# One hybrid decoder layer on one core: causal attention taken in pairs of heads, score products alternating between the two 64-row halves of the array, and the same for the GLA state products

## The chip, the cores and the metric

The kernel runs on one core of a Trainium2 chip. The metric is the device time of one launch in microseconds. The kernel before takes 718.95 us, the median of three runs (718.24 to 720.07).

## What is computed

One decoder layer on 512 tokens of width 1024, all in float32 at the interface. What the change touches are two of its parts; both read the same RMS-normed input:

```python
# 8 attention heads of width 64, causal, blocks of 256 keys, T5 bias by distance
s_own = einsum('hqd,hld->hql', qi, k_own) * scale + table_t[:, rel_bucket(d_own)]
...
p = softmax(concatenate([s_sel, s_own], axis=-1))
o_a = einsum(p_sel, v_sel) + einsum(p_own, v_own)
# 4 heads of gated linear attention: key width 64, value width 128
o_inter = einsum('bhcd,bhde->bhce', qf * exp(b), S)
o_intra = einsum('bhij,bhje->bhie', A, vf)
o_g = rms_norm(o_inter + o_intra, g_norm) * silu(rg)
x = x + concatenate([o_a, o_g]) @ w_out
```

With 512 tokens and blocks of 256, every past block is chosen, so the attention is plain causal attention. After it come an output projection with a residual sum, cross-attention over 256 memory tokens, and a squared-ReLU MLP, none of which the change touches.

## The kernel before, in words

Dense products are made in three passes of half-precision parts (high by high, high by low, low by high), each a matmul of 128 rows by up to 512 columns (`gemm_steps`, L227 to L229, and `gemm_tok_steps`, L242 to L244). One step of such a product is three matmuls. TensorE's order is the order of the program text; the other engines' instructions are ordered by the framework's own planner.

To keep TensorE busy while other engines work between dependent products, independent products are kept in a queue of generators, `fill`, and `fill(n)` issues n steps of them. Where a dependent product stands in TensorE's order is thus set by the number of fill steps written ahead of it.

**GLA** (class `Gla`) works on the four heads in two pairs. Head hh of a pair lies in rows 64 hh to 64 hh + 63 of the pair's tiles. For each head `outp` makes the output of four token tiles J in one PSUM bank: a float32 product of 128 rows with the local matrix `adg` (L643), and for J > 0 a float32 product of 64 rows with the state handed on, `st` (L645). A float32 product shows as two matmul instructions in the trace. The squares go to ScalarE (L647), and `norm` sums them with a matmul (L652), takes the root through `rstd_neg2`, and scales the output (L656). The loop calls, for each head, `outp`, four fill steps, `norm`, three fill steps. Earlier, `small`, `mid` and `large` (L562, L571, L580) make the local matrices with small products whose position alternates between the two row halves.

**Attention.** `Head` works on one head. It loads the bias rows (L723) and spreads them with GpSimd (L724). `score(qt)` makes the scores of one block of 128 queries against its 128 (qt + 1) keys in one PSUM bank: three matmuls of 64 rows (L732 to L734). Then VectorE adds the bias and takes the row maximum (L737, L738), and ScalarE the exponentials with their sum (L740). After the blocks 2 and 0, `parts` splits two blocks of probabilities into half-precision parts, high on ScalarE (L759), low on VectorE (L760). When all four are there, `trans` issues one transposing DMA for the head (L764). Two heads later `attn_out(p)` (L775) multiplies the transposed probabilities of the two heads of pair p with the values, in matmuls of 128 rows by 64 columns that alternate between the two column halves; `split` (L273, L274) puts the result into `mix[p]`.

The main loop (L828 to L851) runs over the heads: the query blocks 3, 2, 1, 0 with one fill step after each (two from the second head on, for g > 0), then `trans`; after every second head from the fourth on `attn_out` of the pair that is two heads back. The fill queue holds the projections of the later heads (`qk_steps`), the gates (`rg_steps`), and from the ninth round on the first part of the output projection (`early_steps`, which reads `mix[0]`, `mix[1]`, `mix[4]`, `mix[5]`) and the rest of it (`residual_steps`). The last `attn_out` has six early and three more steps ahead of it in the last rounds, and one behind it.

PSUM has five banks for such work (`sbank`, L64) and three for the dense products (`gbank`). The transposed probabilities have three buffers.

Of the kernel before, what the change touches and what calls it, by code (L numbers as in the profile page):

```python
# [9 lines left out]
F16 = mybir.dt.float16  # L10
# [6 lines left out]
P = 128  # L17
# [12 lines left out]
# pairs of tiles (f, f + 16) of the hidden layer in the order they are made, for each half of the second  # L30
# product's contraction: (plain,), or (by seven products, plain alongside or None)
# [7 lines left out]
def hybrid_block_kernel(  # L39
# [10 lines left out]
    # ---------------------------------------------------------------- pools  # L50
# [16 lines left out]
    # ------------------------------------------------------------ constants  # L67
# [16 lines left out]
    # ------------------------------------------------------- weight streams  # L84
    class Weights:
# [16 lines left out]
        def pieces(self, n):  # L102
            """the next weight tile in n column ranges, one at a time"""
# [116 lines left out]
    # matmuls of one output tile, three passes of half-precision parts per K tile  # L220
# [26 lines left out]
    # independent products that fill the tensor engine between dependent ones  # L247
# [28 lines left out]
    # (v y^2 - 3) y = -2 rsqrt(v): one Newton step on y = exp(-ln(v)/2), v = ssq / dim  # L276
# [12 lines left out]
    def norm_steps(xs, n, gcol, dst, c0, ssq, nm, inplace=False, keep=None):  # L289
        """dst[kt][:, h/l, c0:c0+n] = split(xs[kt] * rstd * gain)"""  # L290
# [11 lines left out]
    class SumSq:  # L302
        """sum over the features of the squares, plus 1024 * EPS"""
# [38 lines left out]
    # ------------------------------------------------------ phase-1 storage  # L342
# [13 lines left out]
    # --------------------------------------------------- norms of mem and x  # L356
    # mem * gain is split as it comes; its 1/rms is applied to the products
# [83 lines left out]
    # ------------------------------------------------ GLA input projections  # L441
# [54 lines left out]
    # ------------------------------------------------------------------ GLA  # L496
    class Gla:
# [26 lines left out]
        # blocks of 8 tokens: both exponents are taken from the block's middle  # L524
# [10 lines left out]
        # left half against right half of blocks of 2 s tokens, exponents from the end of the left  # L535
# [65 lines left out]
        # between tiles of 128 tokens  # L601
# [19 lines left out]
        # what the tiles before hand on: st[J] = exp(b at the end) st[J - 1] + kc^T v  # L621
# [14 lines left out]
        def outp(self, hh):  # L636
            h = 2 * self.pr + hh
            ps = self.po = sbank(f"go{h}")
            vc = slice(h * P, h * P + P)
            r = slice(64 * hh, 64 * hh + 64)  # L640
# [5 lines left out]
            self.sq = pg.tile([P, T], F32, tag="gd", bufs=2, name=f"gsq{h}")  # L646
            ACT.activation(self.sq, ps, AF.Square)  # L647

        def norm(self, hh):
            h = 2 * self.pr + hh  # L650
            pv = sbank(f"gss{h}")
            PE.matmul(pv, ones, self.sq, start=True, stop=True)  # L652
# [3 lines left out]
            DVE.scalar_tensor_tensor(mixf[4 + h], self.po, gneg[:, G_GN:G_GN + 1], w, op0=ALU.mult, op1=ALU.mult)  # L656
# [3 lines left out]
    # --------------------------------------------------------------- T5 bias  # L660
    # vector over distances, copied to 128 rows of DRAM that shift by one each
# [21 lines left out]
    for pr in range(2):  # L683
# [31 lines left out]
    # ----------------------------------------------------- causal attention  # L715
# [3 lines left out]
    class Head:  # L719
        def __init__(self, h):  # L720
            self.h, self.r, self.pr = h, slice(64 * (h % 2), 64 * (h % 2) + 64), {}
            bq = self.bq = p1.tile([P, T], F32, tag="bq", bufs=3, name=f"bq{h}")
            nc.sync.dma_start(bq[:, 256:], bscr[h, :, 127:383])  # L723
# [24 lines left out]
        def parts(self, qt):  # L748
            # key block kt of query block qt lies at qt + 3 kt, the last one at 7
            if qt == 3:  # L750
                self.pq = pt.tile([P, 2, 10, P], F16, tag="pq", bufs=2, name=f"pq{self.h}")
# [590 lines left out]
```

## Time and profile before

| What | Value |
|---|---|
| Runs | 718.24, 718.95, 720.07 us |
| Span of the profiled execution, first to last instruction | 715.9 us |
| Time of the profiled execution beyond its span | not listed; the median is 3.0 us above the span |
| TensorE busy | 693.4 us, 97% of the span |
| VectorE busy | 553.9 us, 77% |
| ScalarE busy | 419.6 us, 59% |
| GpSimd busy | 84.5 us, 12% |
| Granted TensorE clock, mean | 0.989 of full speed |
| Share of the chain that ended last on TensorE | 81% |

The share of the chain says which engine the end waited for; the busy share says only how often an engine had work. A stretch of matmuls is read best from the starts in the timeline: the time from one start to the next is what a matmul takes from the stream, while its own duration also holds the way through the array, which the next one overlaps.

### The profile page before, as it was taken

Reading aid. Unit: us, or ns where it says so; the run is one execution under the profiler, and the core shown is the slowest. Engines: PE = TensorE matmul, PEld = TensorE weight load, DVE = VectorE, ACT = ScalarE, POOL = GpSimd, SP = SyncE. Lnnn points to the kernel's source line nnn. Section 1 sums busy time; section 2 is a strip of 40 time slices with the busy share of each in tenths; the row PEclk is TensorE's granted clock in tenths of the full one; section 3 lists DMA queues with packets and bytes.
Section 4 is the critical chain, followed back from the end, with each engine's and each line's share of the span. In section 5 each row is a group of like instructions: output and inputs, shape, how many; then the busy total and the mean of one; then the engine's idle time right before and its main releaser. Section 6 shows DMA issues by size and latency. Waiting matters only on the chain.

```text
span 715.9 us, 13482 instructions
## 1 busy us (share of the span) xinstructions
PE 693.4 (97%) x5370; PEld 473.8 (66%) x5370; DVE 553.9 (77%) x1003; ACT 419.6 (59%) x803; POOL 84.5 (12%) x97
## 2 busy tenths in 40 slices
PE   6997999999999999999999999999999999999995
PEld 3843455554333488788888854458888866488884
DVE  7899762747889918857639899889878889999825
ACT  6686544538888617455536666555444766665533
POOL 5701000200110024200124100000000000003211
PEclk8999999999999999999999999999999999999998
DMA  8766623006585903326403332203333342314003
GB/s 315 253 215 206 253 80 103 2 2 224 129 185 132 248 33 119 118 60 177 104 16 122 115 108 70 89 30 119 118 122 114 122 165 70 117 49 139 21 1 119
DMA packets 56628, 85.63 MB, mean 120 GB/s; under 512 B 32075, under 2 KB 37492, under 8 KB 56564
## 3 DMA queue, kind: packets, MB, share of 16 engines
q1 hardware_dynamic: 56564, 84.76, 38.1%
q8 instruction: 42, 0.69, 0.4%
q14 instruction: 22, 0.18, 0.1%
HBM read 75.30 MB, written 3.68 MB: 110 GB/s over the span
## 4 chain that ended last, share of the span: by engine, by line
PE 81%; DVE 11%; ACT 3%; issue 2%; DMA 1%; POOL 1%; DVEq 0%; SPq 0%; ACTq 0%; POOLq 0%
PE up L228 6%; PE up L229 6%; PE up L227 6%; PE a L1116 4%; PE a L1118 4%; PE a L1117 4%; DVE whl L115 3%; PE qk L227 2%; PE qk L229 2%; PE qk L228 2%; PE xq L227 2%; PE xq L229 2%; PE xq L228 2%; PE c L1117 2%; PE c L1118 2%
## 5 line engine op out<-in xcount | busy, mean ns | idle before, releaser
L115 DVE SCALAR_TENSOR_TENSOR whl<-wst,whl 128x1024 f16<-128x1024 f32 (+1 forms) x162 | 197.5, 1226 | 32.1 <-ACT whl L114 31.6
L114 ACT ACTIVATE whl<-wst 128x1024 f16<-128x1024 f32 (+1 forms) x162 | 165.6, 1028 | 33.1 <-PE a L1118 8.0
L227 PEld LDWEIGHTS <-whl 128*128 128x128 f16 x784 | 77.0, 98 | 47.8 <-issue 9.6
L229 PEld LDWEIGHTS <-whl 128*128 128x128 f16 x784 | 77.0, 98 | 46.6 <-DVE whl L115 3.3
L228 PEld LDWEIGHTS <-whl 128*128 128x128 f16 x784 | 77.2, 98 | 36.4 <-issue 1.0
L227 PE MATMUL up<-act,whl 128*128 128x512 f16 (+1 forms) x224 | 78.1, 349 | 0.0
L228 PE MATMUL up<-act,whl 128*128 128x512 f16 (+1 forms) x224 | 78.1, 349 | 0.0
L229 PE MATMUL up<-act,whl 128*128 128x512 f16 (+1 forms) x224 | 78.1, 349 | 0.0
L1116 PE MATMUL a<-t,whl 128*128 128x256 f16 x192 | 52.3, 273 | 1.1 <-ACT v L1133 1.1
L1118 PE MATMUL a<-t,whl 128*128 128x256 f16 x192 | 52.3, 273 | 0.0
L1117 PE MATMUL a<-t,whl 128*128 128x256 f16 x192 | 52.3, 273 | 0.0
L1117 PEld LDWEIGHTS <-whl 128*128 128x128 f16 x456 | 44.6, 98 | 6.9 <-issue 1.5
L1116 PEld LDWEIGHTS <-whl 128*128 128x128 f16 x456 | 44.6, 98 | 5.2
L1118 PEld LDWEIGHTS <-whl 128*128 128x128 f16 x456 | 44.6, 98 | 5.0
L228 PE MATMUL xq<-act,whl 128*128 128x256 f16 x128 | 34.9, 273 | 0.2 <-DVE act L274 0.2
L228 PE MATMUL xo<-ox,whl 128*128 128x256 f16 x128 | 34.9, 273 | 0.0
L227 PE MATMUL xo<-ox,whl 128*128 128x256 f16 x128 | 34.9, 273 | 0.0
L229 PE MATMUL xo<-ox,whl 128*128 128x256 f16 x128 | 34.9, 273 | 0.0
L227 PE MATMUL xq<-act,whl 128*128 128x256 f16 x128 | 34.9, 273 | 0.0
L229 PE MATMUL xq<-act,whl 128*128 128x256 f16 x128 | 34.9, 273 | 0.0
L273 ACT ACTIVATE t<-hs 128x512 f16<-128x512 f32 x32 | 19.8, 624 | 23.9 <-DVE hs L998 23.7
L321 POOL TENSOR_SCALAR accf<-accf 128x128 f32<-128x128 f32 (+1 forms) x3 | 3.5, 1166 | 249.5 <-ACT accf L311 249.5
(339 smaller groups left out, 1722.4 us busy)
## 6 DMA issues: line engine op xcount, KB each, us to landing
wst<-in_w_up SPq DMA_DIRECT2D x32, 512.0 KB, 3.8
wst<-in_w_down SPq DMA_DIRECT2D x32, 512.0 KB, 4.1
wst<-in_w_tt SPq DMA_DIRECT2D x16, 512.0 KB, 4.1
wst<-in_w_xv SPq DMA_DIRECT2D x8, 512.0 KB, 5.2
wst<-in_w_vv SPq DMA_DIRECT2D x8, 512.0 KB, 4.3
wst<-in_w_out SPq DMA_DIRECT2D x8, 512.0 KB, 3.8
wst<-in_w_xq SPq DMA_DIRECT2D x8, 512.0 KB, 3.8
wst<-in_w_xo SPq DMA_DIRECT2D x8, 512.0 KB, 4.6
```

The source lines that it names most:

```text
L114: ACT.activation(wt[:, 0, c], stg[:, c], AF.Copy, scale=SW)
L115: DVE.scalar_tensor_tensor(wt[:, 1, c], stg[:, c], SW, wt[:, 0, c], op0=ALU.mult, op1=ALU.subtract)
L227: PE.matmul(ps, wt[:, 0, kt, :], a[:, 0, c0:c1], start=st, stop=False, **kw)
L228: PE.matmul(ps, wt[:, 0, kt, :], a[:, 1, c0:c1], start=False, stop=False, **kw)
L229: PE.matmul(ps, wt[:, 1, kt, :], a[:, 0, c0:c1], start=False, stop=sp, **kw)
L273: ACT.activation(dst_h, src, AF.Copy, scale=scale)
L321: POOL.tensor_scalar(self.acc, self.acc, 1024 * EPS / P, None, op0=ALU.add)
L1116: PE.matmul(ps, w[:, 0, kt, :], b[:, 0, c], start=st, stop=False, skip_group_check=not start)
L1117: PE.matmul(ps, w[:, 0, kt, :], b[:, 1, c], start=False, stop=False, skip_group_check=not start)
L1118: PE.matmul(ps, w[:, 1, kt, :], b[:, 0, c], start=False, stop=sp, skip_group_check=not start)
```

## The change

`Gla.outp` makes both heads of a pair in one call: first all eight products with `adg` (128 rows), then the six with the state, J by J, the two heads in turn, in two banks. The fill steps around it are regrouped: six behind `outp`, four behind each `norm`, so 14 for a pair as before. In the attention, `Head` becomes `Pair`: for a query block the three score passes of the two heads alternate between the row halves, in two PSUM banks. The small operations on the maxima and sums work on two columns at once. Scores and probabilities share one buffer for each query block. The bias tile of a pair moves to another pool. `trans` issues two transposing DMAs, one behind the other. Between the query blocks stand two fill steps where there was one for each head; two more follow `trans`; and `attn_out` of a pair comes within the next pair's round, behind its third query block.

```diff
-        def outp(self, hh):
-            ps = self.po = sbank(f"go{h}")
...
-            for J in range(4):
-                o = ps[:, J * P:J * P + P]
-                PE.matmul(o, vg[J][:, vc], self.adg[:, hh * 4 + J, :], start=True, stop=(J == 0))
-                if J > 0:
-                    PE.matmul(o, self.st[r, J * P - P:J * P], self.qb[r, J * P - P:J * P], start=False, stop=True)
+        def outp(self):
+            self.po = [sbank(f"go{2 * self.pr + hh}") for hh in range(2)]
+            for hh in range(2):
+                h = 2 * self.pr + hh
+                for J in range(4):
+                    PE.matmul(self.po[hh][:, J * P:J * P + P], vg[J][:, h * P:h * P + P], self.adg[:, hh * 4 + J, :],
+                              start=J == 0, stop=False, skip_group_check=True)
+            for J in range(1, 4):
+                for hh in range(2):
+                    r = slice(64 * hh, 64 * hh + 64)
+                    PE.matmul(self.po[hh][:, J * P:J * P + P], self.st[r, J * P - P:J * P], self.qb[r, J * P - P:J * P],
+                              start=False, stop=J == 3, skip_group_check=True)
...
+        G.outp()
+        fill(6)
         for hh in range(2):
-            G.outp(hh)
+            G.norm(hh)
             fill(4)
-            G.norm(hh)
-            fill(3)
...
-    class Head:
+    class Pair:
...
+            bq = self.bq = pt.tile([P, 2, T], F32, tag="bq", bufs=2, name=f"bq{p}")
...
         def score(self, qt):
-            ps = sbank(f"s{h}_{qt}")[:, :n]
-            PE.matmul(ps, aq[p][r, 0, qs], ak[p][r, 0, :n], start=True, stop=False)
-            PE.matmul(ps, aq[p][r, 0, qs], ak[p][r, 1, :n], start=False, stop=False)
-            PE.matmul(ps, aq[p][r, 1, qs], ak[p][r, 0, :n], start=False, stop=True)
+            pss = [sbank(f"s{p}_{qt}_{hh}")[:, :n] for hh in range(2)]
+            for i, (a, b) in enumerate(((0, 0), (0, 1), (1, 0))):
+                for hh, ps in enumerate(pss):
+                    r = slice(64 * hh, 64 * hh + 64)
+                    PE.matmul(ps, aq[p][r, a, qs], ak[p][r, b, :n], start=i == 0, stop=i == 2)
...
+                self.pq = [pt.tile([P, 2, 10, P], F16, tag="pq", bufs=3, name=f"pq{self.p}_{hh}") for hh in range(2)]
...
         def trans(self):
+            self.ph = []
+            for hh in range(2):
+                pT = pt.tile([P, 20, P], F16, tag="pT", bufs=3, name=f"pT{self.p}_{hh}")
+                nc.sync.dma_start(pT, self.pq[hh].rearrange("p s n t -> p (s n t)"), transpose=True)
...
-    for i in range(10):
+    for i in range(5):
...
         for g in range(4):
-            if i < 8:
-                heads[i].score(3 - g)
-                fill(1)
-            if g > 0 and 1 <= i <= 8:
-                fill(1 if i < 8 else 2)
-        if i < 8:
-            heads[i].trans()
-        if i == 9:
-            fill(3)
-        if i >= 3 and i % 2 == 1:
-            p = (i - 3) // 2
-            attn_out(p, [heads.pop(2 * p), heads.pop(2 * p + 1)])
-            fill(1)
+            if i < 4:
+                pairs[i].score(3 - g)
+                fill(2)
+            if g > 0 and i >= 1:
+                fill(2 if i < 4 else 4)
+            if 1 <= i < 4 and g == 2:
+                attn_out(pairs.pop(i - 1))
+        if i < 4:
+            pairs[i].trans()
+            fill(2)
+    fill(3)
+    attn_out(pairs.pop(3))
+    fill(1)
```

## Rows read from the trace of the kernel before

**Rows 1.** The page's first part: busy time and instructions of each engine.

```profile
PE 693.4 (97%) x5370; PEld 473.8 (66%) x5370; DVE 553.9 (77%) x1003; ACT 419.6 (59%) x803; POOL 84.5 (12%) x97
```

**Rows 2.** Busy time by stretch (start:end, length, engines, PEclk, DMA share, GB/s): the attention.

```profile
175.00:250.00 75.00, 75.00 (x416) 29.93 (x416) 67.95 (x213) 58.84 (x140) 3.72 (x5) 1.00 0.74 181
```

**Rows 3.** TensorE's timeline (start, duration, what) around the first `outp`, then L643's durations.

```profile
117.31 0.38 PE L244 MATMUL va<-whl,act 128*128 128x512 f16 x1
117.53 0.61 PE L643 MATMUL go<-adg,vgs 128*128 128x128 f32 x4
118.06 0.49 PE L645 MATMUL go<-qb,st 64*128 64x128 f32 x2
118.48 0.49 PE L643 MATMUL go<-adg,vgs 128*128 128x128 f32 x2
...
120.15 0.39 PE L242 MATMUL va<-whl,act 128*128 128x512 f16 x1
...
L643 PE MATMUL go<-adg,vgs x32: 273/275/377, 117.5 to 168.2; 128*128 128x128 f32 x32
```

**Rows 4.** TensorE's timeline through the four score groups of the first head.

```profile
174.69 0.38 PE L229 MATMUL qk<-act,whl 128*128 128x512 f16 x1
175.00 0.39 PE L732 MATMUL s<-qks,qks 64*128 64x512 f16 x1
...
175.75 0.39 PE L227 MATMUL qk<-act,whl 128*128 128x512 f16 x1
...
176.19 0.38 PE L229 MATMUL qk<-act,whl 128*128 128x512 f16 x1
...
177.09 0.39 PE L227 MATMUL qk<-act,whl 128*128 128x512 f16 x1
...
177.54 0.38 PE L229 MATMUL qk<-act,whl 128*128 128x512 f16 x1
...
178.28 0.39 PE L227 MATMUL qk<-act,whl 128*128 128x512 f16 x1
...
178.72 0.38 PE L229 MATMUL qk<-act,whl 128*128 128x512 f16 x1
...
179.30 0.39 PE L227 MATMUL qk<-act,whl 128*128 128x512 f16 x1
```

**Rows 5.** TensorE's timeline, matmuls begun within 0.02 and 0.01 us: alternating row halves, column halves.

```profile
102.06 0.27 PE L580 MATMUL ps<-z 64*64 64x64 f32 x2
...
201.05 0.41 PE L775 MATMUL o<-pT,vas 128*64 128x512 f16 x2
```

**Rows 6.** Softmax chain by tile: count, duration min/median/max in ns, first and last start.

```profile
L740 ACT ACTIVATE p<-ss,sm x32: 384/553/723, 179.2 to 235.0; 128x512 f32<-128x512 f32 x8, 128x384 f32<-128x384 f32 x8, 128x256 f32<-128x256 f32 x8, 128x128 f32<-128x128 f32 x8
...
L759 ACT ACTIVATE pq<-p,sm x40: 384/502/616, 182.5 to 239.0; 128x384 f16<-128x384 f32 x16, 128x128 f16<-128x128 f32 x16, 128x256 f16<-128x256 f32 x8
...
L764 SPq DMA_TRANSPOSE pT<-pq x8: 3017/3284/4232, 185.3 to 240.5; - x8
...
DMA to landing us min/median/max: 4.9/5.4/6.6
```

**Rows 7.** Timeline: last score groups of the sixth and eighth head, their transposes, the last `attn_out`.

```profile
215.88 0.23 PE L732 MATMUL s<-qks,qks 64*128 64x128 f16 x1
...
220.13 3.02 SPq L764 DMA_TRANSPOSE pT<-pq  x1
...
232.38 0.23 PE L732 MATMUL s<-qks,qks 64*128 64x128 f16 x1
...
240.47 4.23 SPq L764 DMA_TRANSPOSE pT<-pq  x1
...
247.56 0.41 PE L775 MATMUL o<-pT,vas 128*64 128x512 f16 x2
```

**Rows 8.** Busy time by stretch (columns of rows 2): a long wait of TensorE, and the stretch behind it.

```profile
58.20:62.20 4.00, 0.51 (x11) 0.18 (x11) 4.00 (x8) 3.23 (x5) 0.00 (x0) 1.00 0.77 262
62.20:65.60 3.40, 3.10 (x19) 0.76 (x17) 3.40 (x5) 2.65 (x5) 0.00 (x0) 0.50 0.38 114
```

More of the change, by code (lines that the diff above doesn't have):

```diff
@@ L651, in norm @@
             pv = sbank(f"gss{h}")
-            PE.matmul(pv, ones, self.sq, start=True, stop=True)
+            PE.matmul(pv, ones, self.sq[hh], start=True, stop=True)
             v = pg.tile([P, T], F32, tag="gd", bufs=2, name=f"gv{h}")
@@ L655, in norm @@
             w = rstd_neg2(v, T, 1.0, f"g{h}")
-            DVE.scalar_tensor_tensor(mixf[4 + h], self.po, gneg[:, G_GN:G_GN + 1], w, op0=ALU.mult, op1=ALU.mult)
+            DVE.scalar_tensor_tensor(mixf[4 + h], self.po[hh], gneg[:, G_GN:G_GN + 1], w, op0=ALU.mult, op1=ALU.mult)
     for _ in gqk_steps(0):
@@ L717, in hybrid_block_kernel, with __init__ @@
     pt = s3.enter_context(tc.tile_pool(name="patt", bufs=1, reuse_waits="tile"))
-    class Head:
[L720 to L723, printed above, removed]
-            POOL.tensor_copy(bq[:, :256], bq[:, 256:257].to_broadcast([P, 256]))
-            self.sm = pt.tile([P, 12], F32, tag="sm4", bufs=3, name=f"sm4_{h}")
+    class Pair:
+        def __init__(self, p):
+            self.p, self.pr = p, {}
+            bq = self.bq = pt.tile([P, 2, T], F32, tag="bq", bufs=2, name=f"bq{p}")
+            for hh in range(2):
+                nc.sync.dma_start(bq[:, hh, 256:], bscr[2 * p + hh, :, 127:383])
+                POOL.tensor_copy(bq[:, hh, :256], bq[:, hh, 256:257].to_broadcast([P, 256]))
+            self.sm = pt.tile([P, 3, 4, 2], F32, tag="sm4", bufs=2, name=f"sm4_{p}")
@@ L735, in score @@
-            s = pt.tile([P, T], F32, tag="s", bufs=3, name=f"ss{h}_{qt}")[:, :n]
-            mx, ng, sm = (self.sm[:, 4 * i + qt:4 * i + qt + 1] for i in range(3))
-            DVE.tensor_tensor_reduce(s, ps, self.bq[:, T - n:], scale=1.0, scalar=NEG, op0=ALU.add, op1=ALU.max, accum_out=mx)
+            for i, (a, b) in enumerate(((0, 0), (0, 1), (1, 0))):
+                for hh, ps in enumerate(pss):
+                    r = slice(64 * hh, 64 * hh + 64)
+                    PE.matmul(ps, aq[p][r, a, qs], ak[p][r, b, :n], start=i == 0, stop=i == 2)
@@ L738, in score @@
+            mx, ng, sm = (self.sm[:, i, qt, :] for i in range(3))
+            for hh, ps in enumerate(pss):
+                s = self.pr[qt, hh] = pt.tile([P, n], F32, tag=f"p{qt}", bufs=2, name=f"p{p}_{qt}_{hh}")
+                DVE.tensor_tensor_reduce(s, ps, self.bq[:, hh, T - n:], scale=1.0, scalar=NEG, op0=ALU.add, op1=ALU.max, accum_out=mx[:, hh:hh + 1])
             DVE.tensor_scalar(ng, mx, -1.0 / (SA * SA), None, op0=ALU.mult)
-            pr = self.pr[qt] = pt.tile([P, T], F32, tag="p", bufs=4, name=f"p{h}_{qt}")[:, :n]
@@ L740, in score @@
-            ACT.activation(pr, s, AF.Exp, bias=ng, scale=1.0 / (SA * SA), accum_out=sm)
+            for hh in range(2):
+                s = self.pr[qt, hh]
+                ACT.activation(s, s, AF.Exp, bias=ng[:, hh:hh + 1], scale=1.0 / (SA * SA), accum_out=sm[:, hh:hh + 1])
             if qt % 2 == 0:
-                r = self.sm[:, 8 + qt:10 + qt]
+                r = self.sm[:, 2, qt:qt + 2, :]
                 DVE.reciprocal(r, r)
@@ L775, in attn_out @@
                     PE.matmul(ps[64 * hh:64 * hh + 64, P * kt:T], va[kt][:, a, 64 * h:64 * h + 64],
-                              heads[hh].ph[:, b, offs[kt]:offs[kt] + n],
+                              pair.ph[hh][:, b, offs[kt]:offs[kt] + n],
                               start=(kt == 0 and a == 0 and b == 0), stop=(kt == 3 and a == 1),
@@ L827, in hybrid_block_kernel @@
     fill.add(qk_steps(2), qk_steps(3), *[rg_steps(h) for h in range(4)])
-    heads = {}
-    for i in range(10):
-        if i < 8:
-            heads[i] = Head(i)
-        if i in (4, 6):
-            fill.until({4: 5, 6: 4}[i])
-        if i == 8:
+    pairs = {}
+    for i in range(5):
+        if i < 4:
+            pairs[i] = Pair(i)
+        if i in (2, 3):
+            fill.until({2: 5, 3: 4}[i])
+        if i == 4:
             fill.drain()
```

39 lines of the change are left out of this document (19 added, 20 removed).

## The prediction

> **What bounds the kernel now.** I read the page's first part first: TensorE is busy 693.4 us of a span of 715.9 [rows 1]. An engine that is never idle is shortened only by taking work out of its stream, so the question is what its stream holds in the two stages touched, and whether the other engines can keep up when it gets shorter. The row of the attention stretch shows TensorE busy in all of 75 us, at a granted clock of 1.00 (2.4 GHz), with VectorE at 67.95 and ScalarE at 58.84 [rows 2]: TensorE sets the pace, but VectorE is 9% behind it. Then the timeline of TensorE, read by starts. A step of the dense products takes 0.22 us a matmul, 0.65 for its three. Around the first `outp` the starts run unevenly [rows 3]: four instructions of one kind, then pairs that change between 128 and 64 rows. Around each score group there is more time than three matmuls need [rows 4].
>
> **What goes out of TensorE's stream: GLA.** One `outp` takes from the dense matmul at 117.31 to the next at 120.15, 2.84 us, less the dense matmul's own 0.22: 2.62 for a head, 5.24 for a pair [rows 3]. Within one kind an instruction takes (0.61 - 0.275) / 3 = 0.11 us. The stretch 118.06 to 118.48 holds two instructions in 0.42 us, so going into a 64-row stretch and out of it costs 0.42 - 0.22 = 0.20 beside the products; the first four take 0.53, 0.09 over 4 x 0.11. The new order of a pair is 16 instructions of L643 (1.76 and 0.09), then the 12 of L645 as six pairs in which both row halves run at once (0.66), and one passage through a 64-row stretch (0.20): 2.71. A pair saves 2.53, the two pairs 5.1. If the halves run one after the other, it is 0.66 more for each pair, and 3.7 in all.
>
> **Scores.** The four groups of a head take 1.06, 0.90, 0.74 and 0.58 us from the dense matmul before to the one behind; less 0.22 each, that is 0.84, 0.68, 0.52 and 0.36, 2.40 for a head and 19.2 for eight [rows 4]. The matmuls of a head are 3 x 1280 columns; at 0.22 us for 512 that is 1.65, so 0.75 goes into the eight changes between 128 and 64 rows. If the two halves run at once, a pair costs what a head does now: 9.6 in all, a saving of 9.6. If not, only the changes are halved: 3.0. That halves run at once has its nearest row in `large`: two matmuls on the two row halves begin within 0.02 us, as two on the column halves of L775 do within 0.01 [rows 5]. I take that, 9.6 and 5.1, together 14.7.
>
> On the page "TensorE: Matmul & The Clock Gate", section "Measured speedup vs the span model", the Trainium skill gives 3.07 for four row tiles instead of 4. Rows 5 show no such loss at the start of a pair. By that rule two halves would gain about 1.54, an estimate from that page, and the sum would be some 2 us smaller.
>
> **What the change puts in: a wait for the transposes.** `attn_out(p)` needs both transposes of its pair. TensorE's order is written out, so everything behind a waiting `attn_out` waits too: the fill steps, the next score group, and through it VectorE and ScalarE. I count what lies ahead of it. For pair 0, from its first score group: 20 fill steps of 0.65 (13.0) and seven groups (2.40 + 0.84 + 0.68 + 0.52 = 4.44) make 17.4 us. For the transposes: the first exponential came 4.2 us after the first group at 175.0 (179.2), VectorE being busy with GLA's last norm. From there ScalarE has, for two heads, 8 exponentials at 0.553 and 10 splits at 0.50: 9.4 us [rows 6]. So the first transpose is issued at 13.6. Its issue holds the queue for 3.3; the second follows at 16.9 and lands 5.4 later [rows 6], at 22.3. That is 4.9 us after TensorE comes. If the first transpose misses the last split of the other head (0.5), it is 4.4; if a projection's split and a weight tile come between, by the median and the longest instruction of rows 6 or more, about 6.5. I take 5.
>
> For the others I count from the last score group of the pair. Pairs 1 and 2 have 16 steps (10.4) and 0.36 + 2.04 of groups: 12.8. Pair 3 has 27 steps: 17.9. Before, the transpose of one head was issued 4.2 us (215.88 to 220.13) to 8.1 us (232.38 to 240.47) after that group [rows 7]. The second head adds an exponential and two splits, about 1.3 us by the shorter values of rows 6, of which the first transpose can miss the last 0.4; then 3.3 and 5.4. From 4.2 + 0.9 + 8.7 = 13.8 to 8.1 + 1.3 + 8.7 = 18.1, so pairs 1 and 2 wait 1.0 to 5.3 each and pair 3 up to 0.2. A wait of `attn_out(p - 1)` stands between two groups of pair p and lets ScalarE and VectorE catch up, so pair 1 is near the low end (1.0); in pair 2's rounds the gates add work on both engines (3). The waits together: 5 + 1 + 3 + 0 = 9. The low end is 4.4, where pair 0's wait lets the others catch up for good; the high end 6.5 + 5.3 + 5.3 + 0.2 = 17.3.
>
> **The clock.** The row of the wait before L457 shows TensorE busy for 0.51 of 4.0 us, and the next 3.4 us at a granted clock of 0.50, the lower level of 1.2 GHz [rows 8]. A wait of 5 us can bring that once: half of 3.4 is 1.7. It makes TensorE later and so shortens the next wait; I take 1.0, with ends of 0 and 5.1 (three times). The Trainium skill speaks against long waits in the same way ("TensorE: Matmul & The Clock Gate", "HAM oscillation"): idle gaps between bursts of matmuls bring the lower clock back. Rows 8 agree.
>
> **The rest.** Both norms of a pair now follow each other after four fill steps, where 7 steps and an `outp` lay between; a tail of 0 to 1.5 us may show at the next pair's small products or at the second score group, whose bank GLA's last norm frees. Cover is the fill steps; I take 0.5. The bias loads move to a pool that overlaps GLA's; their place was that of tiles used early, so 0, and if not, the load would add its few microseconds to pair 0's wait. On SP the second transpose stands ahead of later bias and weight loads; the weights are loaded several tiles ahead, 5 us of fill each, so 0. GpSimd's copies keep their number: 0. `mix[3]` has one dense step behind the last `attn_out` where six early steps lay; with two of the other residual steps that is as long as ScalarE and VectorE need: 0, at most 1. On VectorE fewer small operations: hidden.
>
> **Sum.** 14.7 - 9 - 1 - 0.5 = 4.2 less. On the span that is 715.9 to 711.7; the profiled execution's own time isn't listed, and its span is 3.0 below the median of the runs, so the median goes from 718.95 to 714.8.
>
> **Rivals.** A, the forecast: 714.8, its own range 711 to 719, chance 0.45.
>
> B, the waits are hidden: the planner puts the softmax of the older pair first and TensorE meets landed transposes. 718.95 - 14.7 + 0.5 = 704.8. For it: before, no `attn_out` waited. Against: 13.6 + 3.3 + 5.4 for pair 0 against 17.4 hardly bends. 0.10.
>
> C, slower: the same waits near their upper ends. Pair 0 waits 6.5, pairs 1 and 2 up to 5.3, each long enough to bring the lower clock; 17.3 + 3.4 for two such stretches + 0.5 is 21.2, 6.5 more than is saved: 725. It decides from 14.7 + 2.2 on, so when waits and clock together pass 17 us. For it: the lag of 8.1 us in row 240.47. Against: a wait gives the other engines time, so three long ones in a row are unlikely. 0.20, at 722 to 725.
>
> D, VectorE becomes the bound: it has 67.95 us of work in the stretch. Were it to work without a break and with 2 us of waiting for ScalarE, the stretch would go from 75 to 70 and the attention would gain 5 of its 9.6, with GLA's 5.1 and little waiting beside: 708.9. The Trainium skill has this as a rule ("TensorEngine Tiling (Array Packing)", "PSUM Bottleneck"): tiling speeds up the array and not the reading of PSUM. 0.15.
>
> E, the change doesn't do what it says: the halves run one after the other. 3.7 + 3.0 = 6.7 saved; TensorE comes 1.6 us later to each `attn_out`, so the waits fall to 3.4 + 0 + 1.4, and with 0.5 the time is 717.5. Rows 5 speak against it. 0.10.
>
> **How the numbers follow.** The time is that of A. A measurement of this kernel tells about 0.3%, 2.2 us, from no change. Faster than 716.8: seven tenths of A (0.32), B, D and a third of E: 0.60. Slower than 721.1: C and a little of A: 0.22. The rest 0.18. The range leaves out B, and the slower part of C: 707.5 to 723.
>
> **What would show it.** In the changed profile: score groups of six matmuls whose two halves start within 0.02 us, and 0.84 us from dense step to dense step at 512 columns (E wrong); an `outp` of a pair of 2.7; TensorE idle before L775's successor, released by the DMA of `pT`, 5 us for pair 0 and less after; a stretch at clock 0.50 behind it. Wrong would be: no such wait (B or D), waits of over 5 us more than once (C), or half starts 0.2 us apart (E).

## The result, and the profile after

The changed kernel takes 723.37 us, the median of four runs (722.87 to 724.54), against 718.93 for the kernel before: a ratio of 1.0057, interval [1.0042, 1.0073]. It is slower by 4.4 us, where 714.8 was forecast.

**What went as worked out.** First the page's first part and its chain, and TensorE's timeline through one pair's `outp` and one score block.

```profile
PE 686.4 (95%) x5370; PEld 472.7 (66%) x5370; DVE 551.3 (76%) x971; ACT 417.8 (58%) x803; POOL 81.7 (11%) x97
...
PE 55%; DVE 9%; ACT 3%; issue 2%; POOL 1%; DMA 1%; DVEq 0%; ACTq 0%; POOLq 0%
```

```profile
118.63 0.38 PE L244 MATMUL va<-whl,act 128*128 128x512 f16 x1
118.85 1.95 PE L642 MATMUL go<-adg,vgs 128*128 128x128 f32 x16
120.73 0.94 PE L647 MATMUL go<-qb,st 64*128 64x128 f32 x12
121.60 0.39 PE L242 MATMUL va<-whl,act 128*128 128x512 f16 x1
...
170.96 0.38 PE L229 MATMUL qk<-act,whl 128*128 128x512 f16 x1
171.27 0.82 PE L744 MATMUL s<-qks,qks 64*128 64x512 f16 x6
172.03 0.39 PE L227 MATMUL qk<-act,whl 128*128 128x512 f16 x1
```

TensorE is busy 7.0 us less than before [rows 1] in a span that is 5.2 longer: there is less work, and more waiting. The 55% in the chain can't be set against the 81% before, since these shares sum to 71%: the chain was followed back only to 216.19 us. The `outp` of a pair takes from 118.63 to 121.60 less the dense matmul's own 0.22, so 2.75, where 2.71 was worked out. Six score matmuls of 512 columns take 0.76 from their start to the next dense one, as three did [rows 4]: the halves run beside each other.

**Where the time went.** The row of attention, from the first score product to the first matmul that sums the squares of the output projection (`ssqout`), first in the kernel before, then in the changed one with its two stretches at the lower clock. Columns as in [rows 2], the engines in the order of [rows 1].

```profile
175.00:271.90 96.90, 96.90 (x599) 47.84 (x599) 72.58 (x223) 63.02 (x149) 9.65 (x13) 1.00 0.59 148
```

```profile
171.30:277.00 105.70, 93.17 (x599) 49.13 (x599) 71.42 (x193) 62.62 (x150) 9.48 (x16) 0.94 0.54 135
179.70:183.10 3.40, 3.40 (x17) 1.06 (x14) 2.24 (x12) 2.35 (x7) 0.19 (x1) 0.50 0.02 8
196.80:207.00 10.20, 6.38 (x35) 3.44 (x36) 4.12 (x13) 4.08 (x12) 0.00 (x0) 0.50 0.64 165
```

The same 599 matmuls took 96.90 us without a gap; now they take 105.70. TensorE stood idle for 105.70 - 93.17 = 12.5. At a granted clock of 0.50 it was busy for 3.40 + 6.38 us, and half of that, 4.9, is what the lower clock cost. What is left, 93.17 - 4.9 = 88.3, is the work at full clock: 8.6 less than before, where 9.6 was counted. So attention is longer by 12.5 + 4.9 - 8.6 = 8.8. In GLA, from the first `go` product to the first score product, 57.47 us (117.53 to 175.00) became 52.42 (118.85 to 171.27), 5.05 less. The two make 3.8 of the 4.4. (Every run has some stretches at the lower clock in its first 70 us, of varying length, and its first `go` comes at 117.5 to 121.5 us; the comparisons below leave that part out where they can.)

**Which waits.** The waits of TensorE, and its timeline where they stand (the bracket gives the idle time and what ended it).

```profile
PE o L791 <- DMA pT<-pq: 8.6, 4, 3.3
...
PE s L744 <- DVE sm L748: 2.4, 1, 2.4
...
PE s L744 <- DVE mix L662: 1.4, 1, 1.4
```

```profile
176.88 0.28 PE L744 MATMUL s<-qks,qks 64*128 64x256 f16 x1 [1.40 <-DVE mix L662]
179.59 0.70 PE L744 MATMUL s<-qks,qks 64*128 64x256 f16 x5 [2.43 <-DVE sm L748]
...
197.35 0.63 PE L791 MATMUL o<-pT,vas 128*64 128x512 f16 x1 [2.74 <-DMA pT<-pq]
201.25 3.04 PE L791 MATMUL o<-pT,vas 128*64 128x512 f16 x20 [3.27 <-DMA pT<-pq]
...
219.44 1.79 PE L791 MATMUL o<-pT,vas 128*64 128x512 f16 x23 [0.51 <-DMA pT<-pq]
...
256.57 1.79 PE L791 MATMUL o<-pT,vas 128*64 128x512 f16 x23 [2.11 <-DMA pT<-pq]
```

Pair 0's product waits twice, once for each head's transpose, 6.0 together; pair 1 waits 0.5, pair 2 has no such entry, pair 3 waits 2.1. Ahead of them the third score block of pair 0 waits 1.40 and 2.43 for its banks. A wait that the prediction did not have is the one for the bank of the first bias sum (L748). Its cause stands in the timelines of SP's queue, GpSimd, VectorE and ScalarE, and beside them in SP's and VectorE's of the kernel before.

```profile
165.48 7.39 SPq L113 DMA_DIRECT2D wst<-in_w_out  x4
172.96 1.81 SPq L732 DMA_DIRECT2D bq<-bscr  x4
...
178.41 1.47 POOL L733 COPY bq<-bq 128x256 f32<-128x256 f32 x4 [42.20 <-DMA bq<-bscr]
...
178.84 0.69 DVE L748 CUSTOM_DVE_ANT_0 p<-s,bq 128x512 f32<-128x512 f32 x1 [2.02 <-POOL bq L733]
...
180.75 0.72 ACT L752 ACTIVATE p<-p,sm 128x512 f32<-128x512 f32 x1 [6.70 <-DVE sm L749]
```

```profile
95.39 0.42 SPq L723 DMA_DIRECT2D bq<-bscr  x1
...
113.70 0.43 SPq L723 DMA_DIRECT2D bq<-bscr  x1
...
177.78 0.68 DVE L737 CUSTOM_DVE_ANT_0 ss<-s,bq 128x512 f32<-128x512 f32 x1
```

The bias rows of the first pairs are issued at 172.96, behind weight loads, land over 5 us later, and are spread by GpSimd from 178.41; only then, 7.6 us after the first score product, VectorE adds the first bias. In the kernel before three of these loads were issued between 95 and 114 us and the first sum came 2.8 us after the first score product.

The chain that ended last tells what the later rounds waited for. From 216.19 us to pair 3's product it holds 26.1 us of VectorE, 6.8 of ScalarE and 4.9 of the last transpose, and nothing of TensorE; in the kernel before it is TensorE's alone from 175 to 272. Its last pieces:

```profile
251.36 0.27 DVE rge L807
251.63 4.90 DMA pT<-pq
...
256.57 0.38 PE o L791
```

### The profile page after: what moved, and what is told of

The parts are those of the page before. It is cut to its first block, busy times and chain, and to the rows that moved or that the text cites. A ratio compares the mean times of both kernels' runs of the same rounds, so it can differ in the third digit from the quotient of the medians.

```text
span 721.1 us, 13438 instructions
## 1 busy us (share of the span) xinstructions
PE 686.4 (95%) x5370; PEld 472.7 (66%) x5370; DVE 551.3 (76%) x971; ACT 417.8 (58%) x803; POOL 81.7 (11%) x97
## 4 chain that ended last, share of the span: by engine, by line
PE 55%; DVE 9%; ACT 3%; issue 2%; POOL 1%; DMA 1%; DVEq 0%; ACTq 0%; POOLq 0%
PE up L229 6%; PE up L227 6%; PE up L228 6%; PE a L1132 4%; PE a L1134 4%; PE a L1133 4%; DVE whl L115 2%; PE xq L229 2%; PE xq L228 2%; PE xq L227 2%; PE c L1132 2%; PE c L1133 2%; PE c L1134 2%; PE xo L229 1%; PE xo L228 1%
## 5 line engine op out<-in xcount | busy, mean ns | idle before, releaser
L227 PE MATMUL out<-mix,whl 128*128 128x256 f16 (+1 forms) x112 | 32.2, 288 | 0.0
```

Of the source, the lines that this page charges most:

```text
L227: PE.matmul(ps, wt[:, 0, kt, :], a[:, 0, c0:c1], start=st, stop=False, **kw)
```

## The experiments

Three theories went into them: that waits and the lower clock behind them took the gain back (W); that matmuls on half the array lower the clock by themselves (H); and that VectorE and ScalarE, not TensorE, set the pace of attention (V). All ratios are against the kernel before, measured in the same series. Lengths called "attention" go from the first score product to the first `ssqout`, 96.90 before and 105.70 after.

**1. The GLA part alone, on the kernel before**: `outp` for a pair and its fill steps as in the change's diff; attention as before.

> The kernel before with the GLA part of the change alone (both heads in one outp, fill steps regrouped), the attention as before. Theory W (the change saves what it was costed at, and what makes it slower are waits of TensorE in the attention and the lower clock behind them): 5.0 us faster than before, about 713.9, an outp of a pair at 2.7 us, granted clock 1.00 from 110 to 250 us, no new wait over 0.5 us. Theory H (products on alternating halves fill the array less, and that itself lowers the clock): a stretch at clock 0.50 near the outp, and less than 3 us gained. Theory V (VectorE and ScalarE set the pace of the attention, so time saved ahead of it is lost there): within 1 us of before.

716.23 us (714.90 to 717.81), ratio 0.9945 [0.9927, 0.9963]. The first `go` to the first score product takes 52.75 us, attention 97.30, and no stretch of attention is at the lower clock. The first of these was 57.47: 4.7 of the 5.1 arrive there, 4.0 in the time (0.55% of 719). Half-array products bring no lower clock by themselves: H has nothing for it here.

**2. The attention part alone**: the changed kernel with GLA's `outp`, `norm` and fill steps of before, the reverse of the first edit.

> The attention part of the change alone, GLA as before. If the parts add up: the GLA part gave 720.57 to 716.23, so 4.3 us; the attention part alone is 723.4 + 4.3 = 727.7, some 8 us over the kernel before, with the waits for pT of pair 0 near 6 us. If the earlier arrival at attention (5 us from GLA) had been what made the bias rows late, the attention part alone loses less: 720 to 724.

726.69 us, 1.0093 [1.0080, 1.0107]. The parts add within their intervals: 0.9945 + 1.0093 - 1 = 1.0038 beside the measured 1.0057. The whole loss is the attention part's; arriving earlier from GLA is not what makes it.

**3. The bias rows from a pool that is free earlier.**

```diff
-            bq = self.bq = pt.tile([P, 2, T], F32, tag="bq", bufs=2, name=f"bq{p}")
+            self.bq = []
             for hh in range(2):
-                nc.sync.dma_start(bq[:, hh, 256:], bscr[2 * p + hh, :, 127:383])
+                bq = p1.tile([P, T], F32, tag="bq", bufs=3, name=f"bq{p}_{hh}")
+                nc.sync.dma_start(bq[:, 256:], bscr[2 * p + hh, :, 127:383])
```

> The changed kernel with the bias rows of each head in the earlier pool again (three buffers of one head), so that their loads stand ahead of the output weights on SP's queue. Theory W: VectorE's first bias sum comes within 3.5 us of the first score group instead of 7.6, the waits of TensorE at the score groups (3.8 us) and the first stretch at clock 0.50 (3.4 us long, 1.7 us of cost) are gone; the wait for pair 0's transposes stays at 5 to 7, with the second stretch behind it: 718 to 719. Theory H: the stretches at 0.50 stay where score groups are, and the time is 720 or more. Theory V: 722 to 723.5.

720.23 us (718.82 to 722.31), 0.9997 [0.9986, 1.0007]: 4.3 us of the loss is gone (1.0057 - 0.9997 of 719). The loads are issued from 96.86 on, and the first bias sum comes 4.8 us after the first score product instead of 7.6. But the waits for `pT` are 9.8 in four; what was saved ahead of pair 0's product is partly waited there. The profiled run was the slowest of the twelve, and its attention, 104.54, is only 1.2 us shorter than the changed kernel's, so where the rest is gained is not shown.

**4. `attn_out` behind the next pair's transposes and two fill steps**, and not between its third and fourth score block.

```diff
-            if 1 <= i < 4 and g == 2:
-                attn_out(pairs.pop(i - 1))
         if i < 4:
             pairs[i].trans()
             fill(2)
+        if 1 <= i < 4:
+            attn_out(pairs.pop(i - 1))
```

> The changed kernel with attn_out of a pair behind the next pair's trans and its two fill steps instead of behind its third query block: six fill steps and a score group later, 4.3 us. Theory W: pair 0's wait falls from 6.0 to about 1.7, pairs 1 and 2 have none, the last one (2.1) stays; the ten microseconds at clock 0.50 behind pair 0's wait are gone, the first stretch (3.4) stays: 723.4 - 4.3 - 5 = 714, up to 716. Theory H: the waits shrink and the stretches at 0.50 stay: 719. Theory V: the time moves by less than 1 us, as another wait takes their place.

715.84 us (714.27 to 718.34), 0.9942 [0.9922, 0.9962]. Nothing of the arithmetic differs from the changed kernel, only where one call stands, and the time falls by 1.15%. Its waits and its row of attention:

```profile
PE o L791 <- DMA pT<-pq: 2.9, 2, 2.2
...
PE s L744 <- DVE sm L748: 2.0, 1, 2.0
...
PE s L744 <- DVE mix L662: 1.4, 1, 1.4
```

```profile
172.32:268.79 96.47, 89.61 (x598) 47.18 (x598) 71.23 (x193) 61.71 (x150) 9.95 (x16) 0.98 0.59 148
```

A wait of 8.6 for `pT` became 2.9. The last score block of the pair that is being worked on no longer stands behind the waiting product.

**5. TensorE kept busy in pair 0's waits**: 18 unused dense matmuls ahead of its third score block, 28 ahead of its `attn_out`. They are additional work; nothing reads their bank.

```diff
+                if (i, g) == (0, 2):
+                    busy(18)
                 pairs[i].score(3 - g)
...
             if 1 <= i < 4 and g == 2:
+                if i == 1:
+                    busy(28)
                 attn_out(pairs.pop(i - 1))
```

> The changed kernel with matmuls that compute nothing needed (128 by 512, into a spare bank) put where TensorE waits: 18 (3.9 us) ahead of pair 0's third score group, 28 (6.0 us) ahead of pair 0's attn_out. Theory W: the clock stays at 1.00 through the attention; the waits are as long as before but filled, so only the cost of the lower clock goes: 5 to 6.8 us less, at most 1 us of it given back where the filling is longer than the wait: 717 to 719. Theory H: stretches at 0.50 stay: 723 or more. Theory V: as W for the clock, but the time stays within 1 us of 723.4 since VectorE and ScalarE end when they did.

724.54 us (723.77 to 725.85), 1.0061 [1.0045, 1.0078]: as the changed kernel. Only one stretch of 3.4 us (202.1 to 205.5) is at the lower clock, where there were 13.6; the score blocks wait for no bank. The gain is given back by the later pairs:

```profile
PE o L796 <- DMA pT<-pq: 7.4, 4, 3.4
```

```profile
172.00:278.83 106.83, 99.43 (x645) 52.66 (x644) 71.73 (x193) 62.73 (x150) 9.70 (x16) 0.98 0.54 133
```

Pair 2 now waits 2.0 and pair 3 3.4, where they waited 0 and 2.1. What the clock takes and what the waits take is not a sum of two losses: while TensorE is slow, the softmax goes on, and the next product waits less. This speaks against W as I stated it and for V: how soon the other engines bring the transposed probabilities sets the time.

**6. Edits 3 and 4 together.**

> The changed kernel with both earlier edits at once: the bias rows of a head in a pool whose buffers are free earlier, and each attention product moved behind the next pair's transposes and two fill steps. If the two delays were separate stretches on the path, their gains add: 723.4 - 3.1 (bias) - 7.5 (product later) = about 712.8, and PE waits for pT and for the score banks together below 3 us. If both only shorten the same chain (scores, maxima, exponentials, transposes, product), the second gives nothing on top of the better one: 715 to 716.

710.77 us (709.82 to 712.78), 0.9867 [0.9853, 0.9882]: at least the sum of the two (1.0057 less 0.0060 and 0.0115 is 0.9882). One wait for `pT` is left, 2.6 us in pair 0, with 3.4 us at half clock behind it.

```profile
172.94:266.49 93.55, 89.23 (x599) 47.64 (x598) 72.05 (x194) 62.52 (x151) 8.93 (x13) 0.98 0.61 154
```

**7. `attn_out` later still**, behind the second score block two rounds on (three score blocks later than in the changed kernel), with four buffers of `pT` (two of `pq`) and early bias rows.

```diff
-            if 1 <= i < 4 and g == 2:
-                attn_out(pairs.pop(i - 1))
+            if i >= 2 and g == 1:
+                attn_out(pairs.pop(i - 2))
```

> The changed kernel with early bias rows and each attention product moved by three score groups, into the next round behind its third group (four buffers of pT, two of pq). Theory of the chain: the product is then never early, PE waits for pT go to 0, no stretch below full clock lies in attention, and all of the 14.7 us counted in the prediction is left: 718.9 - 14.7 = 704 to 707 at best, if the third pair's product does not hold up the output projection. Rival, VectorE sets attention's pace: what PE saves comes back as waits of the score products for their banks, time as with the shorter delay, 712 to 716.

714.98 us (713.43 to 717.85), 0.9933 [0.9917, 0.9948]. Both expectations have their half. The waits for `pT` are 0.6 and nothing of attention is at the lower clock, so the score products of pairs do not lower it by themselves either (H). But score blocks wait 4.2 in six places and the output projection 1.9 for a gate's split. A longer distance isn't better without end; what the smaller number of `pq` buffers adds to these waits was not parted.

**8. The score products of one head together again**, those of the second head behind them.

```diff
-            for i, (a, b) in enumerate(((0, 0), (0, 1), (1, 0))):
-                for hh, ps in enumerate(pss):
+            for hh, ps in enumerate(pss):
+                for i, (a, b) in enumerate(((0, 0), (0, 1), (1, 0))):
```

> The changed kernel with one edit: the three score products of a head stand together again, those of the second head behind them, so that no two halves run beside each other; banks, waits and order of all else stay. By the trace this costs PE 6.4 us (half of 48 products of 0.267 us). Theory of the chain: that time lies beside the waits for pT and the bias sums, 723 to 725, with the waits shorter by about what PE is longer. Rival, attention is bound by PE's products: 723.4 + 6.4 = 729.8.

720.59 us (717.02 to 721.47), 1.0003 [0.9993, 1.0014]: 3.9 us faster than the changed kernel (1.0057 - 1.0003 of 719), which neither theory had. The edit doesn't do what I took it for. The timeline:

```profile
172.26 0.38 PE L229 MATMUL qk<-act,whl 128*128 128x512 f16 x1
172.57 0.83 PE L744 MATMUL s<-qks,qks 64*128 64x512 f16 x6
173.33 0.39 PE L227 MATMUL qk<-act,whl 128*128 128x512 f16 x1
```

The six take 0.76 us, as they do in turns: the halves still run beside each other. The same view cut off at 172.60 shows two of them begun, together 0.40 long where one alone is 0.39:

```profile
172.57 0.40 PE L744 MATMUL s<-qks,qks 64*128 64x512 f16 x2
```

That the order was changed all the same shows in pair 0's third block, where the banks came late: three run, then the other three, and not one and five as above.

```profile
178.18 0.50 PE L744 MATMUL s<-qks,qks 64*128 64x256 f16 x3 [1.38 <-DVE mix L662]
180.62 0.48 PE L744 MATMUL s<-qks,qks 64*128 64x256 f16 x3 [1.94 <-DVE sm L748]
```

So this is no test of concurrency, and the 3.9 come from elsewhere. Pair 3's transposes are issued at 244.3, 17.7 us after pair 2's, and its product does not wait; in the changed kernel that is 21.5 us, with a wait of 2.1. Also the lower clock holds for 6.8 us of attention and not for 13.6. Experiment 10 follows the first up.

**9. The same edit on the kernel of experiment 6.**

> The best kernel so far (early bias rows, product behind the next pair's transposes, 710.8) with the three score products of a head together again, so that the two halves do not run beside each other. In the changed kernel this edit did not cost its 6.4 us (half of 48 products of 0.267) but gained 2.8. If TensorE's stream sets the pace once the waits are gone, it costs the 6.4 here: 717.2. If the other engines still set it, it costs under 2: 711 to 712.5.

711.95 us (710.20 to 712.62), 0.9882 [0.9865, 0.9900], not told apart from 0.9867 [0.9853, 0.9882]. With the halves running together in either order there was nothing to lose; the expectation rested on the same mistake.

**10. Softmax ahead of other ready work on VectorE and ScalarE, for pair 3 alone.** The planner orders these engines; `high_priority` tells it to put the bias sums, exponentials and splits of that pair first. TensorE's order stays.

```diff
+            with (tc.high_priority() if p == 3 else ExitStack()):
...
                 DVE.tensor_tensor_reduce(s, ps, self.bq[:, hh, T - n:], scale=1.0, scalar=NEG, op0=ALU.add, op1=ALU.max, accum_out=mx[:, hh:hh + 1])
```

> The changed kernel with one edit that moves no product and no bank: for the last pair alone the planner is told to put the bias sums, exponentials and splits ahead of other ready work on VectorE and ScalarE. In VectorE's order 7 gate operations then stand ahead of the pair's last split, where 13 stood (10 in the kernel with the halves one after the other). Theory of the planner's order: the two transposes of pair 3 are issued 3 to 4 us sooner after those of pair 2 (21.5 us before), the wait of 2.1 us for pair 3 goes: 721 to 721.5. Rival, the transposes are late because of the products ahead: no change, 723 to 724.

720.93 us (719.70 to 724.61), 1.0020 [1.0005, 1.0035]. VectorE's groups between the first transpose of pair 2 and that of pair 3, first in the changed kernel, then here (L803 and L804 are the first operation of a gate), with the row of that stretch:

```profile
L807 DVE SCALAR_TENSOR_TENSOR rge<-rge,rgu 128x512 f32<-128x512 f32 x3 | 2.1, 686 | 0.0
...
L803 DVE TENSOR_SCALAR rge<-rge 128x512 f32<-128x512 f32 x3 | 1.3, 421 | 0.1
...
226.36:247.86 21.50, 21.43 (x125) 9.84 (x124) 20.42 (x54) 18.74 (x43) 0.00 (x0) 1.00 0.70 177
```

```profile
L808 DVE SCALAR_TENSOR_TENSOR rge<-rge,rgu 128x512 f32<-128x512 f32 x2 | 1.4, 686 | 0.1
L804 DVE TENSOR_SCALAR rge<-rge 128x512 f32<-128x512 f32 x2 | 0.8, 410 | 0.0
...
225.29:241.35 16.06, 16.06 (x102) 7.48 (x101) 15.12 (x45) 14.37 (x37) 0.00 (x0) 1.00 0.70 174
```

VectorE is busy 20.42 of 21.50 us in the one and 15.12 of 16.06 in the other: in this stretch it has no room, and whatever the planner puts ahead of the last splits moves the transposes. The changed kernel has work of a third gate there. With that put back, pair 3's wait is gone, and the time is 2.7 us less (1.0057 - 1.0020 of 719). Not all of it is that wait: in the profiles attention is 3.3 us shorter (102.36), 1.9 of it between pair 2's product and pair 3's. The other 1.4 lie ahead of that, where the edit puts nothing first; there the lower clock holds for 6.8 us and not for 13.6, though pair 0 waits 7.3 and not 6.0.

**11. The same for all pairs**, in the changed kernel.

> The same for all four pairs: bias sums, exponentials and splits ahead of other ready work; TensorE's order as in the changed kernel. Theory of the chain: the waits for pT (8.6 us in four) fall to those of pair 0 alone, 4 to 5, one stretch at the lower clock stays: 717 to 719.5. Rival, VectorE has too much work in all and what is put back (projections' splits, gates) stops TensorE elsewhere: 722 to 725, with new waits at the dense products or at the scores.

722.13 us, 1.0022 [1.0009, 1.0035]: no more than for pair 3 alone. The waits for `pT` are still 7.5 in four (pair 0: 5.6), two stretches of 6.8 us each are at the lower clock, the banks still wait 4.0, 2.6 of it for the late bias rows. Both expectations are missed in part: the waits did not shrink to those of pair 0, and none came up at the dense products. With the bias rows late and the product close behind, the order of VectorE did little for pair 0.

**12. The same for all pairs, on the kernel of experiment 6.**

> The best kernel so far with the softmax put first for all pairs as well. Its one wait for pT (2.64 us, pair 0) and the stretch of 3.4 us at half clock behind it would go: 710.8 - 2.6 - 1.7 = 706.5 at best. Rival, work that is put back stops TensorE at the output projection, whose first part needs the first two gates: 711 to 714.

714.76 us (711.85 to 716.82), 0.9922 [0.9900, 0.9945]: about as the rival had it. No stretch of attention is at the lower clock, but TensorE stands 1.6 and 1.4 us at the output projection, for splits of the gates that were put back.

**13. The halves really apart**: one of the two dense steps behind a score block put between the two heads, on the kernel of experiment 6.

```diff
             for hh, ps in enumerate(pss):
+                if hh == 1:
+                    fill(1)
                 for i, (a, b) in enumerate(((0, 0), (0, 1), (1, 0))):
...
                 pairs[i].score(3 - g)
-                fill(2)
+                fill(1)
```

> The fastest kernel so far (early bias rows, product behind the next pair's transposes, 710.8) with one of the two dense steps that stood behind a score block put between the two heads' products, so that they can't run beside each other and each head has its own way from 128 to 64 rows and back: 9.6 us more of TensorE's stream by the prediction's count (19.2 instead of 9.6). The earlier edit that only changed the written order did not separate them: the trace shows the second head's matmuls 0.010 us behind the first head's all the same. If TensorE sets the pace once the waits are short: 710.8 + 9.6 = 720.4, less the waits that this hides (2.6 for pT, 1.7 for the banks, 1.7 of clock), so 714.5 to 720.4. If the other engines set the pace, 710.5 to 712.

715.41 us (714.76 to 716.34), 0.9940 [0.9926, 0.9954], against 0.9867 [0.9853, 0.9882]: what running side by side is worth there, with the changes between 128 and 64 rows that it saves, is 0.73%, 5.2 us. Its row and a block of it:

```profile
171.47:269.04 97.57, 97.02 (x599) 48.25 (x598) 71.88 (x194) 62.91 (x151) 9.01 (x13) 1.00 0.58 147
```

```profile
171.47 0.82 PE L748 MATMUL s<-qks,qks 64*128 64x512 f16 x3
172.22 0.39 PE L227 MATMUL qk<-act,whl 128*128 128x512 f16 x1
...
172.97 0.82 PE L748 MATMUL s<-qks,qks 64*128 64x512 f16 x3
173.72 0.39 PE L227 MATMUL qk<-act,whl 128*128 128x512 f16 x1
```

Three matmuls take the 0.75 that six took, and TensorE is busy 97.02 of 97.57, with all the work of the kernel before (96.90). So with its waits hidden the structure in pairs costs 0.7 us by itself, 0.5 of it a last wait for `pT`, and the halves running together is worth 97.57 - 93.55 = 4.0 of attention.

**14. The same separation in the changed kernel itself.**

> The same separation in the changed kernel itself. TensorE's stream is 9.6 us longer; if all that the halves save is given back to the waits and the lower clock, the time stays: 722 to 724.5, with the waits for pT and banks (12.4 us) and the loss to the clock (6) shorter by about 9. If products and waits add up: 733.

724.92 us (723.97 to 725.48), 1.0068 [1.0054, 1.0082], beside 1.0057 [1.0042, 1.0073]: the two are not told apart. In the changed kernel nearly all of what the halves save is waited away again; the waits at `pT` and the banks fall from 12.4 to 7.1, the stretch at the lower clock from 13.6 to 6.8.

**15. Softmax first for pair 0 alone, on the kernel of experiment 6.**

> The fastest kernel so far with the softmax put first on VectorE and ScalarE for pair 0 alone, the pair of its one wait for pT (2.6 us with 1.7 of half clock behind it). For all pairs this put the gates back, and TensorE stood 3.0 us at the output projection; for pair 0 alone the gates keep their place. Best: 710.8 - 0.6 to 4.3 = 706.5 to 710. If the wait of pair 0 is set by when the first bias sums can start and not by the order, no change: 710 to 711.5.

709.66 us (709.62 to 710.46), 0.9862 [0.9848, 0.9876]. Pair 0's wait falls from 2.6 to 1.2 and the stretch at the lower clock behind it is gone; the interval does not part it from experiment 6. It is the fastest of all, 1.4% under the kernel before.

```profile
172.73:263.99 91.26, 88.12 (x599) 46.79 (x598) 71.50 (x194) 62.16 (x151) 8.24 (x13) 1.00 0.61 157
```

With no clock lost its 88.12 is the work at full clock: 8.8 less than before.

## Why the prediction was wrong

**Right: what goes out of TensorE's stream.** GLA's 5.1 measured 5.05, and with the edit alone 0.55% of the time. That the halves run together (rival E against it) is shown by the blocks of 0.76 us. Read by starts as in the prediction, the four score groups of a pair take 0.84, 0.69, 0.53 and 0.37 us (experiment 5), 2.43 where 2.40 was counted. By TensorE's busy time the scores' 9.6 is 8.6 here and 8.0 to 9.05 in the runs with no clock lost (7, 12, 15). Most of the gap is an effect of counting: ahead of each of six waits a matmul counts with its whole 0.38 and not with the 0.22 from start to start, by estimate 1.0 in all. The prediction scaled the Trainium skill's 3.07 for four row tiles ("TensorE: Matmul & The Clock Gate", "Measured speedup vs the span model") down to 1.54 for two halves. That estimate does not hold here: six matmuls in the time of three are a factor of 2.

**Wrong: the waits, 9 forecast and 12.5 measured.** The waits for `pT` alone are 8.6 beside the 9, but that is luck: pairs 0 and 3 waited 1.0 and 2.1 more than forecast, pairs 1 and 2 3.5 less. The rest are 3.8 at the banks. Under it lies the form of the sum: it took TensorE for the pace of attention and subtracted waits counted one by one, where the chain from 216 us on is VectorE's and ScalarE's, and what TensorE saves turns into waits (experiment 14). Three steps failed.

- "their place was that of tiles used early, so 0", on the bias loads. They were issued at 172.96 instead of from 95 on. The first exponential came 9.5 us after the first score product (180.75), not 4.2, and the second transpose landed 30.0 after it, not 22.3. That pair 0 waits 6.0 at the product and not 13 is because TensorE had already waited 3.8 at the banks and lost 1.7 to the clock behind them. Experiment 3 puts this step at 4.3 us by the runs' times. The sentence allowed for it ("if not, the load would add its few microseconds to pair 0's wait") but the sum did not.
- "A wait ... lets ScalarE and VectorE catch up". In part it does: pair 1 waited 0.5 where 1 was taken, pair 2 none where 3 was. But a waiting `attn_out` between two score blocks also holds back the block behind it, and so the transposes of that pair. With the call moved behind all four blocks the time fell by 8.3 us (experiment 4, 1.0057 to 0.9942), the waits for `pT` by 5.7 and the time at the lower clock from 13.6 to 3.4; that edit gives the transposes more time as well, and how much is due to either was not parted.
- Pair 3's 0. It waited 2.1, because the planner put work of a third gate ahead of the last splits in a stretch where VectorE is busy 95%. Experiment 10 shows it: without that work the wait is gone, and about 2 of its 2.7 us lie there.

**Mis-sized: the clock, 1.0 forecast.** Two stretches of 3.4 and 10.2 us cost 4.9. I had worked from one stretch of 3.4 [rows 8], with three of them as the upper end (5.1). But experiment 5 shows that this term is no cause of its own: with only 3.4 us at the lower clock left, the time was the same. The sum had 10.5 for waits, clock and the rest (GLA's tail, now the 1.4 at the bank that its last norm frees) and the runs 17.4, which is 6.9 more; the scores' work by busy time adds 1.0 and GLA 0.1. That is 8.0 of the 8.6 between forecast and result.

**The rivals.** C came out, in time (723.4 in 722 to 725) and in its condition: it decides when waits and clock pass 17, and 12.5 + 4.9 is 17.4. Its way was another: it had three long waits for `pT`, where there were one long one, a medium one and a wait for banks, so the hit is in part luck. I gave it 0.20 because "a wait gives the other engines time"; the runs show that TensorE's saved time in attention is almost all turned into waits when the product stands that close (experiment 14). B and E fell. D was right in part: VectorE is not busy throughout (71.4 of 105.7 us), but from 216 us to pair 3's transposes it holds most of the chain. With the waits short, the halves' 9.6 are worth 4 to 5 us (experiment 13), near the 5 that D had; what bounds that kernel then was not parted.

## What to carry to other kernels

Work saved on the engine that was never idle was worth here only the distance that the products behind it still have to their inputs: count, for each dependent product in a written-out order, what lies ahead of it and what its input's own chain takes, and move the product before judging the saving. A wait inside a round also holds the work that feeds the next input: count that work too (what it cost by itself was not parted here). When a tile moves to another pool, look up when the memory under it comes free and what its load then stands behind on the queue.

## What the runs showed of the hardware

Matmuls on the two row halves run beside each other even when three of one half stand in the program ahead of the three of the other (0.76 us for the six, experiment 8); a dense step between them parts them (experiment 13). The Trainium skill says that matmuls stay in program order ("TensorE: Matmul & The Clock Gate", "The mechanism"). Here the first matmul of the second half starts 0.010 us behind the first of the first half, ahead of the second and third of that half in the order of the program; the measurement decides.

The length of a wait alone does not tell whether the lower clock follows. 3.40 us of idle time brought none in experiment 5, where 1.98 did; 2.74 and 3.27 in a row brought 10.2 us at 1.2 GHz in the changed kernel, 3.12 and 2.69 brought 6.8 in experiment 3, and the longer 3.90 and 3.41 in experiment 10 also 6.8.
